# Attention with float32 probabilities and values, two heads side by side, and the value products of one group handed out between the scores of the next

## The chip, the cores and the metric

The kernel runs on one core of one Trainium2 chip. The metric is the device time of one execution in microseconds (us), the median over several runs. The core's engines are TensorE (PE, with its weight loads PEld), VectorE (DVE), ScalarE (ACT), GpSimd (POOL) and SyncE (SP); each works through its own instructions in a fixed order and waits for semaphores of the others.

## The reference

A chain of four layers over 1024 rows of width 1024. The part that the change touches is attention, in three places:

```
# memory attention (layers 0 and 1): 4 heads of 64, 256 memory rows
s = einsum('bqhd,bmhd->bhqm', q, mk) * HEAD_DIM ** -0.5
p = softmax(s);  out = einsum('bhqm,bmhd->bqhd', p, mv)
# grouped attention of layer 1: 12 query heads, 4 key heads of 64, 1024 rows, no mask
s = einsum('bqhgd,bkhd->bhgqk', qblk, k) * scale
p = softmax(s);  out = einsum('bhgqk,bkhd->bqhgd', p, v)
# latent attention (MLA) of the third layer: 8 heads, causal, 1024 rows, values of 64
s = where(mask, q_nope k_nope + q_rope k_rope, -inf) * scale
p = softmax(s);  out = einsum('bhqk,bkhd->bqhd', p, v)
```

Everything is float32, and the tolerance asks for more than one product in TensorE's rounded float32 format (fp32r in the rows) gives.

## The kernel before

The layers run one after the other: a long-convolution mixer with memory attention (layer 0), its experts, grouped attention with memory attention (layer 1), its experts, a recurrent layer with MLA, and a state-space layer (SSD). Most products are made of fp32r pieces: a number is split into a rounded high part and the rest (`K.split`, L127 to L134: ACT copies the high part, DVE or POOL subtracts), and pieces are multiplied in two or three passes.

**Grouped attention** (`Gqa.attend`, L1414). For each head, two groups of four tiles; a tile is 128 queries by all 1024 keys. Per tile: four score products into a two-bank PSUM tile `gs` (`scores`, L844: twice `gk`, twice `gkl`), the row maximum `mx` on DVE (L873), the exponential `prob` on ACT with the row sums `gsm` (L875), then eight 128x128 transposes `pT` on PE in two halves (L890), each followed by a split into `gph` (ACT) and `gpl` (DVE); one half in eight goes by way of ACT `pc` to POOL. After four tiles `out_heads` (L903) multiplies: values `vst` hold 64 high and 64 low columns side by side, so that one 128-column weight takes both, and per key tile there is one product with `gph` and one with `gpl`, 512 columns each, 16 per group of four tiles into the bank `ov`. ACT copies the two halves out, POOL adds them, and multiplies by `orc`: the reciprocals of the row sums, made rows by four transposes `rT` (L879) and an ACT copy (L921). One DMA stores 64 rows of `mixT`.

**Memory attention** (`Mem.attend`, L814) does the same per pair of heads with 256 columns: four tiles' transposes are split into `mph` and `mpl`, and each head has four products `ov` with `mv`. It stands between the projections of layers 0 and 1.

**MLA** (`Ab.mla_attend`, L1709) goes head by head; of each the four later query tiles, then the four earlier ones. Scores `as` come from three 96-row products and a mask product; the transposes `apT` are split into `aph` and `apl`; `mla_out` (L1776) multiplies with `mlv`, in narrowing column ranges where the mask cuts, and the result is divided by the sums and multiplied by the gate rows `ag` that a DMA has fetched. The splits of each head's queries and keys (`aql`, `akl`) run on POOL from the second head on.

PSUM banks: grouped attention has two for scores of two banks each, three for transposes (`tp`) and one for `ov`; MLA four, three and one. Buffers of the probabilities rotate by two.

The order in which the instructions of independent chains stand on each engine is set by a scheduler, which places them by its own estimates within what the data and the buffers allow; the program's order is its input, not its result. So an edit in the attention code can also move work of the next stage (here the weight pieces `pwh` and `pwl` of the layer's output product, which are prepared during the last heads of MLA).

Of the kernel before, what the change touches and what calls it, by code (L numbers as in the profile page):

```python
# [731 lines left out]
class Mem:  # L732
# [8 lines left out]
    def load(self, pool):  # L741

        K = self.K
        raw = K.raw(4, 256)
        K.nc.sync.dma_start(out=raw, in_=self.d.rearrange("b p n -> p b n"))
        for b in range(2):
            self.key_pair(pool, raw[:, b], 256, f"m{b}")
        self.v = pool.tile([P, 2, 4, P], F32R, name="mv")
        for b in range(2):
            self.values(b, raw[:, 2 + b])  # L750

    def values(self, b, src):
        self.K.split(self.v[:, b, :, 0:64], self.v[:, b, :, 64:128], src.rearrange("p (h d) -> p h d", h=4))

    def kv(self, pool, mt, wp, mem):
# [19 lines left out]
        if not self.layer:  # L775
            self.v = pool.tile([P, 2, 4, P], F32R, name="mv")
# [37 lines left out]
    def attend(self, wk, mixT, row0, pair, qs, tg, pk=None):  # L814

        K = self.K
        ph = wk.tile([P, 4, 256], F32R, name="mph", tag="mph")
        pl = wk.tile([P, 4, 256], F32R, name="mpl", tag="mpl")
        for tt in range(2):
            t = tg * 2 + tt  # L820
            ps = K.psum("ms", "s")
            for q in range(2):
                h = 2 * pair + q
                scores(K, ps[:, q * 256:(q + 1) * 256], qs[q][:, t * P:(t + 1) * P], self.k2[h], self.kl2[h])
            prob = softmax_rows(K, pk or wk, ps[:, 0:512], 2)
            pT(K, prob, ph, pl, tt)
        for q in range(2):
            h = 2 * pair + q
            out_heads(K, wk, ph, pl, [(2 * q + mb, self.v[:, mb, h]) for mb in range(2)],
                      mixT.piece(row0 + h * 64, row0 + h * 64 + 64, tg * 256, (tg + 1) * 256))  # L830
# [48 lines left out]
def columns_to_rows(K, ps, v):  # L879

    for j in range(v.shape[1]):
        K.transpose(ps[0:64, j * P:(j + 1) * P], v[:, j:j + 1].broadcast_to([P, 64]))


def pT(K, prob, ph, pl, tt, pool=None, off=()):

    nc = K.nc
    s = slice(tt * P, (tt + 1) * P)
    for h in range(0, prob.shape[1] // P, 4):
        ps = K.psum("pT", "tp")  # L890
        for k in range(4):
            K.transpose(ps[:, k * P:(k + 1) * P], prob[:, (h + k) * P:(h + k + 1) * P])
        v = ps[:, 0:512].rearrange("p (k t) -> p k t", k=4)
        if h in off:
            c = pool.tile([P, 4, P], F32, name="pc", tag="pc")
            nc.scalar.activation(out=c, in_=v, func=AF.Copy)
            nc.gpsimd.tensor_copy(out=ph[:, h:h + 4, s], in_=c)
            nc.gpsimd.tensor_tensor(out=pl[:, h:h + 4, s], in0=c, in1=ph[:, h:h + 4, s].bitcast(F32), op=OP.subtract)
        else:
            K.split(ph[:, h:h + 4, s], pl[:, h:h + 4, s], v)  # L900


def out_heads(K, pool, ph, pl, kv, dst, tag="tp", sums=None):  # L903

    nc = K.nc
    n = ph.shape[2]
    ps = K.psum("ov", tag)
    for j, (k, v) in enumerate(kv):
        K.mm(ps[:, 0:n], v, ph[:, k], j == 0, False)
        K.mm(ps[:, 0:n], v, pl[:, k], False, j == len(kv) - 1)  # L910
    o = pool.tile([64, n], F32, name="oh", tag="oh")
    nc.scalar.activation(out=o, in_=ps[64:128, 0:n], func=AF.Copy)
    o2 = pool.tile([64, n], F32, name="oh2", tag="oh2")
    nc.scalar.activation(out=o2, in_=ps[0:64, 0:n], func=AF.Copy)  # L914
    nc.gpsimd.tensor_tensor(out=o2, in0=o2, in1=o, op=OP.add)  # L915
    if sums is not None:
        nc.vector.reciprocal(out=sums, in_=sums)
        rp = K.psum("rT", "tp")
        columns_to_rows(K, rp, sums)
        r = pool.tile([64, n], F32, name="orc", tag="orc")  # L920
        nc.scalar.activation(out=r, in_=rp[0:64, 0:n], func=AF.Copy)  # L921
        nc.gpsimd.tensor_tensor(out=o2, in0=o2, in1=r, op=OP.mult)
    nc.sync.dma_start(out=dst, in_=o2)
# [383 lines left out]
class Gqa:  # L1307
# [50 lines left out]
    def results(self, pool, vpool):  # L1358

        self.qT = pool.tile([P, NH // 2, T], F32, name="qT")  # L1360
        self.kT = pool.tile([P, NKV // 2, T], F32, name="kT")
        self.v = vpool.tile([P, NT, NKV, P], F32R, name="vst")
# [5 lines left out]
    def project(self, u, ws, wk, uh, ul, t):  # L1368
# [6 lines left out]
        if u == 1:  # L1375
            p3 = ps[:, 0:256].rearrange("p (h d) -> p h d", h=4)
            K.split(self.v[:, t, :, 0:64], self.v[:, t, :, 64:128], p3)
            return
# [35 lines left out]
    def attend(self, wk, mixT, kpools, qp, op):  # L1414
        K = self.K
        for h in range(NH):
            kv = h // 3
            if h % 3 == 0:
                k2, kl = self.keys(kpools[kv % 2], kv)
            qs = self.stack(qp, h)  # L1420
            for tg in range(2):
                ph = wk.tile([P, 8, 512], F32R, name="gph", tag="gph")
                pl = wk.tile([P, 8, 512], F32R, name="gpl", tag="gpl")
                sm = K.small.tile([P, 4], F32, name="gsm", tag="gsm", bufs=2)
                for tt in range(4):
                    t = tg * 4 + tt
                    ps = K.psum("gs", "s")
                    scores(K, ps, qs[:, t * P:(t + 1) * P], k2, kl)
                    prob = exp_rows(K, wk, ps, sm[:, tt:tt + 1])
                    pT(K, prob, ph, pl, tt, wk, (4,) if tt == 2 else ())  # L1430
                out_heads(K, op, ph, pl, [(kb, self.v[:, kb, kv]) for kb in range(8)],
                          mixT.piece(h * 64, h * 64 + 64, tg * 512, (tg + 1) * 512), tag="ov", sums=sm)
# [81 lines left out]
class Ab:  # L1514
# [157 lines left out]
    def mla_heads(self, pools, rp, wk):  # L1672
# [5 lines left out]
        self.v = pools[2].tile([P, NT, 8, P], F32R, name="mlv")  # L1678
        uqh, uql = load_w(K, rp, a["mla_w_uq_2"][0], 0, 768, 2, "uq")
        ukh, ukl = load_w(K, rp, a["mla_w_ukv_2"][0], 0, 1024, 1, "uk")  # L1680
        for t in range(NT):
# [15 lines left out]
            K.split(self.v[:, t, :, 0:64], self.v[:, t, :, 64:128], v[:, :, 64:128])  # L1697
# [11 lines left out]
    def mla_attend(self, cp, wk, yT):  # L1709
# [7 lines left out]
        G.affine_select(out=msk, in_=z, pattern=[[-1, P]], compare_op=OP.is_ge, fill=-1e30, base=0, channel_multiplier=1)  # L1717
        for h in range(8):
# [4 lines left out]
            pp = []  # L1723
            for tg in range(2):
                pp.append([cp.tile([P, 4 + 4 * tg, 512], F32R, name=f"ap{x}{tg}") for x in "hl"])
            sm = K.small.tile([P, 2, NT], F32, name="asm", tag="asm", bufs=2)
            G.memset(sm[:, 1, 0:4], 0.0)
            todo = [4, 4]
            for t in (4, 5, 6, 7, 0, 1, 2, 3):
                p = self.mla_tile(wk, qk, t, idb, msk, sm)  # L1730
                q = t // 4
                self.mla_pT(p, pp[q], t)
                todo[q] -= 1
                if not todo[q]:
                    self.mla_out(wk, yT, h, q, *pp[q], sm[:, :, 4 * q:4 * q + 4])
# [28 lines left out]
    def mla_pT(self, p, pp, t):  # L1764

        K = self.K
        ph, pl = pp
        cs = slice(t % 4 * P, (t % 4 + 1) * P)
        for k0 in range(0, t + 1, 4):
# [4 lines left out]
            K.split(ph[:, k0:k0 + m, cs], pl[:, k0:k0 + m, cs], tp[:, 0:m * P].rearrange("p (k t) -> p k t", t=P))  # L1774

    def mla_out(self, wk, yT, h, tg, ph, pl, sm):  # L1776

        K, nc = self.K, self.K.nc
        gt = wk.tile([64, 512], F32, name="ag", tag="ag", bufs=1)
        dst = yT.piece(512 + h * 64, 512 + h * 64 + 64, tg * 512, (tg + 1) * 512)  # L1780
        nc.sync.dma_start(out=gt, in_=dst)
        rs = K.small.tile([P, 4], F32, name="ars", tag="ars", bufs=2)
        nc.vector.tensor_tensor(out=rs, in0=sm[:, 0], in1=sm[:, 1], op=OP.add)
        nc.vector.reciprocal(out=rs, in_=rs)
        rp = K.psum("rT", "tp")
        columns_to_rows(K, rp, rs)
        r = wk.tile([64, 512], F32, name="arb", tag="arb", bufs=1)
        nc.scalar.activation(out=r, in_=rp[0:64, 0:512], func=AF.Copy)
        nc.gpsimd.tensor_tensor(out=gt, in0=r, in1=gt, op=OP.mult)
        po = K.psum("ao", "ov")  # L1790
        nk = tg * 4 + 4
        for k in range(nk):
            c0 = max(0, k - tg * 4) * P
            K.mm(po[:, c0:512], self.v[:, k, h], ph[:, k, c0:512], k == 0, False)
            K.mm(po[:, c0:512], self.v[:, k, h], pl[:, k, c0:512], False, k == nk - 1)
        o = wk.tile([64, 512], F32, name="aoh", tag="aoh", bufs=1)
        nc.scalar.activation(out=o, in_=po[64:128, 0:512], func=AF.Copy)
        nc.vector.tensor_tensor(out=o, in0=po[0:64, 0:512], in1=o, op=OP.add)
        nc.gpsimd.tensor_tensor(out=o, in0=o, in1=gt, op=OP.mult)
        nc.sync.dma_start(out=dst, in_=o)  # L1800
# [538 lines left out]
```

## Time and profile before

| | |
|---|---|
| time, median of 3 runs | 3911.36 us (3908.62 to 3912.82) |
| the profiled execution: time | 3914.67 us |
| its span, first to last instruction | 3912.9 us |
| granted clock of TensorE, mean over the span | 0.955 of 2.4 GHz |
| grouped attention | 1624 to 1930 us |
| MLA attention | 2822 to 2984 us |

The page gives busy time per engine over the whole span. Since the stages have different limits, the views of stretches (busy time of each engine between two times) and the timeline of an engine (start, duration, line, operation, tile written <- tiles read, and in brackets the idle time before and what ended it) say more. Matmuls are pipelined: a matmul's recorded duration overlaps the next one, and what a matmul costs is the distance between two starts.

### The profile page before, as it was taken

Reading aid. Unit: us, or ns where it says so; the run is one execution under the profiler, and the core shown is the slowest. Engines: PE = TensorE matmul, PEld = TensorE weight load, DVE = VectorE, ACT = ScalarE, POOL = GpSimd, SP = SyncE. Lnnn points to the kernel's source line nnn. Section 1 sums busy time; section 2 is a strip of 40 time slices with the busy share of each in tenths; the row PEclk is TensorE's granted clock in tenths of the full one; section 3 lists DMA queues with packets and bytes.
Section 4 is the critical chain, followed back from the end, with each engine's and each line's share of the span. In section 5 each row is a group of like instructions: output and inputs, shape, how many; then the busy total and the mean of one; then the engine's idle time right before and its main releaser. Section 6 shows DMA issues by size and latency. Waiting matters only on the chain.

```text
span 3912.9 us, 52838 instructions
## 1 busy us (share of the span) xinstructions
PE 3554.6 (91%) x19679; PEld 3016.3 (77%) x19679; DVE 2877.1 (74%) x5200; ACT 1994.3 (51%) x2958; POOL 1055.1 (27%) x939
## 2 busy tenths in 40 slices
PE   7997999985999979899886999989998998999798
PEld 6885878764988969777766888868786876777577
DVE  6547878857998789777687988766476676667575
ACT  4433532223766754689734767645584234445330
POOL 2004745400453321244301554313352000000010
PEclk9998998997999999999997999989999999999899
DMA  4223333464999951000366999851114312222341
GB/s 156 92 83 109 116 130 113 134 201 169 361 361 355 356 195 34 16 12 12 99 227 230 375 358 346 306 157 48 43 39 128 105 56 81 69 77 92 108 156 65
DMA packets 205721, 603.64 MB, mean 154 GB/s; under 512 B 23110, under 2 KB 114104, under 8 KB 179865
## 3 DMA queue, kind: packets, MB, share of 16 engines
q1 hardware_dynamic: 193769, 558.58, 39.5%
q0 software_dynamic: 11696, 41.69, 4.1%
q8 instruction: 155, 2.54, 0.3%
q14 instruction: 101, 0.83, 0.1%
HBM read 503.60 MB, written 96.60 MB: 153 GB/s over the span
## 4 chain that ended last, share of the span: by engine, by line
PE 60%; DVE 11%; ACT 4%; DMA 2%; issue 2%; POOL 1%; SPq 0%; ACTq 0%; DVEq 0%; POOLq 0%
PE out L176 12%; PE gate L176 8%; PE xbc L176 7%; PE up L176 5%; PE z L176 5%; PE down L176 4%; DVE mwl L134 4%; PE ov L176 2%; PE pT L125 2%; PE gs L176 2%; PE yd L176 2%; PE as L176 1%; PE xr L176 1%; PE qk L176 1%; POOL mwl L134 1%
## 5 line engine op out<-in xcount | busy, mean ns | idle before, releaser
L134 DVE TENSOR_TENSOR mwl<-mwr,mwh 128x1024 fp32r<-128x1024 f32 x486 | 646.3, 1381 | 55.2 <-ACT mwh L130 54.4
L130 ACT ACTIVATE mwh<-mwr 128x1024 fp32r<-128x1024 f32 x576 | 563.0, 1050 | 52.5 <-PE up L176 28.8
L134 POOL TENSOR_TENSOR mwl<-mwr,mwh 128x1024 fp32r<-128x1024 f32 x90 | 257.5, 2887 | 272.2 <-ACT mwh L130 253.9
L1857 POOL DMA_DIRECT2D pyr<-y3T_d x31 | 23.5, 758 | 758.6 <-PE z L176 593.4
L1226 POOL DMA_INDIRECT xg<-xn_d,idx x32 | 58.9, 1839 | 467.2 <-DVE gsc L1224 466.7
L915 POOL TENSOR_TENSOR oh<-oh,oh 64x256 f32<-64x256 f32 (+1 forms) x56 | 55.2, 986 | 396.7 <-ACT oh L914 382.3
L134 DVE TENSOR_TENSOR gpl<-pT,gph 128x512 fp32r<-128x512 f32 x168 | 110.6, 684 | 40.8 <-ACT gph L130 26.8
L873 DVE TENSOR_REDUCE mx<-gs 128x1 f32<-128x1024 f32 x96 | 116.8, 1218 | 30.1 <-PE gs L176 29.8
L125 PE MATMUL pT<-ident,prob 128*128 128x128 f32 x896 | 126.6, 276 | 13.6 <-DVE gpl L134 8.2
L176 PE MATMUL gate<-mwh,xgl 128*128 128x384 f32 x512 | 137.3, 349 | 0.5 <-DVE xgl L134 0.4
L125 PEld LDWEIGHTS pT<-ident,prob 128*128 128x128 f32 x896 | 105.2, 141 | 39.4 <-ACT prob L875 6.7
L176 PE MATMUL gate<-mwl,xgh 128*128 128x384 f32 x512 | 134.7, 343 | 0.9 <-DVE mwl L134 0.8
L176 PE MATMUL gate<-mwh,xgh 128*128 128x384 f32 x512 | 134.2, 342 | 0.0
L176 PE MATMUL up<-mwl,xgh 128*128 128x384 f32 x512 | 132.0, 337 | 1.9 <-DVE mwl L134 1.9
L176 PE MATMUL up<-mwh,xgh 128*128 128x384 f32 x512 | 132.2, 338 | 0.0
L176 PE MATMUL up<-mwh,xgl 128*128 128x384 f32 x512 | 131.6, 337 | 0.0
L176 PE MATMUL down<-mwl,hh 128*128 128x512 f32 x384 | 122.6, 401 | 6.0 <-POOL mwl L134 6.0
L130 ACT ACTIVATE xgh<-xgT 128x512 fp32r<-128x512 f32 (+1 forms) x68 | 38.1, 566 | 173.7 <-PE xgT L125 173.1
L176 PE MATMUL out<-pwh,pyl 128*128 128x512 f32 x384 | 120.8, 396 | 6.3 <-DVE pyl L134 4.9
L176 PE MATMUL down<-mwh,hl 128*128 128x512 f32 x384 | 122.9, 400 | 0.0
L176 PE MATMUL out<-pwl,pyh 128*128 128x512 f32 x384 | 121.1, 396 | 0.0
L176 PE MATMUL out<-pwh,pyh 128*128 128x512 f32 x384 | 121.1, 396 | 0.0
(742 smaller groups left out, 11373.2 us busy)
## 6 DMA issues: line engine op xcount, KB each, us to landing
mwr<-in_exp_w_gate_dram SPq DMA_DIRECT2D x64, 1536.0 KB
mwr<-in_exp_w_up_dram SPq DMA_DIRECT2D x64, 1536.0 KB
mwr<-in_exp_w_down_dram SPq DMA_DIRECT2D x64, 1536.0 KB
csr<-cs_d SPq DMA_DIRECT2D x32, 512.0 KB
raw<-in_ssd_w_in_dram SPq DMA_DIRECT2D x15, 1024.0 KB
k_d<-kev SPq DMA_DIRECT2D x54, 256.0 KB
kt<-k_d SPq DMA_DIRECT2D x54, 256.0 KB
raw<-in_hy_w_in_dram SPq DMA_DIRECT2D x10, 1024.0 KB
```

The lines of the kernel that those rows point to most:

```text
L125: self.nc.tensor.transpose(out, in_, self.ident[:n, :n])
L130: nc.scalar.activation(out=hi, in_=src, func=AF.Copy)
L134: e.tensor_tensor(out=lo, in0=src, in1=hi.bitcast(F32), op=OP.subtract)
L176: self.nc.tensor.matmul(out=out, lhsT=lhsT, rhs=rhs, start=start, stop=stop)
L873: nc.vector.tensor_reduce(out=mx, in_=ps, axis=AX.X, op=OP.max, negate=True)
L915: nc.gpsimd.tensor_tensor(out=o2, in0=o2, in1=o, op=OP.add)
L1226: nc.gpsimd.indirect_dma_start(out=xg, out_offset=None, in_=self.xnD, in_offset=bass.IndirectOffsetOnAxis(ap=idx[:, 0:1], axis=0))
L1857: K.nc.gpsimd.dma_start(out=raw, in_=yT[q].rearrange("(p k) t -> p k t", k=self.kt)[:, :, t * P:(t + 1) * P])
```

## The change

Probabilities and values are no longer split. Values are float32 with 64 columns per head. After a transpose there is one copy: the first half of a grouped-attention tile goes to ACT, the second to DVE; memory attention's go to ACT; MLA's first key half goes to DVE, the other to ACT. The value products are float32 products with 64 weight columns; two heads write the two halves of the same bank (partitions 0 to 63 and 64 to 127), and stand alternately. The sums of a pair of heads are handled once: DVE reciprocal, a POOL copy that spreads them to 128x512 (`orcb`, `arbb`), four transposes, one ACT copy. One DVE multiplication then reads the bank and writes the result, in place of two ACT copies, a POOL addition and a POOL multiplication per head; MLA keeps one POOL multiplication with the gate. One DMA stores the 128 rows of the pair. In the program, the products of a group (two heads, 512 queries) are a generator of eight steps, and one step is taken after each tile of the next group.

```
-def pT(K, prob, ph, pl, tt, pool=None, off=()):
+def pT(K, prob, pt, tt, engs):
...
-            K.split(ph[:, h:h + 4, s], pl[:, h:h + 4, s], v)
+        if engs[h // 4] == "act":
+            nc.scalar.activation(out=pt[:, h:h + 4, s], in_=v, func=AF.Copy)
+        else:
+            nc.vector.tensor_copy(out=pt[:, h:h + 4, s], in_=v)
+def pair_rows(K, pool, sums, tag):
...
+    nc.vector.reciprocal(out=sums, in_=sums)
+    b = pool.tile([P, n, 2, 64], F32, name=tag + "b", tag=tag + "b", bufs=1)
+    nc.gpsimd.tensor_copy(out=b, in_=sums.rearrange("p n (q o) -> p n q o", o=1).broadcast_to([P, n, 2, 64]))
+    rp = K.psum("rT", "tp")
+    for j in range(n):
+        K.transpose(rp[:, j * P:(j + 1) * P], b[:, j].rearrange("p q d -> p (q d)"))
+    r = pool.tile([P, n * P], F32, name=tag, tag=tag)
+    nc.scalar.activation(out=r, in_=rp[:, 0:n * P], func=AF.Copy)
+    return r
-def out_heads(K, pool, ph, pl, kv, dst, tag="tp", sums=None):
+def out_pair(K, pt, vs, tag, done, cut=lambda k: 0):
...
+    for k in range(m):
+        c = cut(k)
+        for q in range(2):
+            K.mm(ps[q * 64:(q + 1) * 64, c:n], vs[q][k], pt[q][k][:, c:n], k == 0, k == m - 1)
+        if k == m - 1:
+            done(ps)
+        yield
 # Gqa.attend
+                for tt in range(4):
                     t = tg * 4 + tt
...
+                    for q in range(2):
+                        ps = K.psum("gs", "s")
+                        scores(K, ps, qs[q][:, t * P:(t + 1) * P], *kk[hs[q] // 3])
+                        prob = exp_rows(K, wk, ps, sm[:, tt, q:q + 1])
+                        pT(K, prob, pt[q], tt, ("act", "dve"))
+                        next(steps, None)
+                finish(steps)
+                steps = self.outputs(op, mixT, pr, tg, hs, pt, sm)
 # Gqa.outputs, once per group
+            r = pair_rows(K, op, sm, "orc")
+            o = op.tile([P, 512], F32, name="oh", tag="oh")
+            K.nc.vector.tensor_tensor(out=o, in0=ps[:, 0:512], in1=r, op=OP.mult)
 # Ab.mla_out
+        r = pair_rows(K, wk, rs, "arb")
         nc.gpsimd.tensor_tensor(out=gt, in0=r, in1=gt, op=OP.mult)
...
+            nc.vector.tensor_tensor(out=o, in0=po[:, 0:512], in1=gt, op=OP.mult)
```

Memory attention calls `out_pair` too and runs all its steps at once, into a `tp` bank, with one ACT copy per pair. `mla_attend` steps the generator twice after each of the earlier query tiles, once after each of the later ones.

What the scheduler makes of this on PE, in the middle of grouped attention (`gs` scores, `pT` transposes, `ov` value products; a row with x is that many in a run). Before, half of a head's products, the next tile and the other half's beginning:

```order
L176 MATMUL ov<-gph,vst 128x512
L176 MATMUL ov<-gpl,vst 128x512
L125 MATMUL pT<-ident,prob 128x128 x4
L176 MATMUL gs<-gk_16408,gqs 128x512 x2
L176 MATMUL gs<-gkl,gqs 128x512 x2
L176 MATMUL ov<-gph,vst 128x512
L125 MATMUL pT<-ident,prob 128x128 x4
L176 MATMUL ov<-gpl,vst 128x512
```

The piece of the changed program at the like place, with the last of 13 products of one group that stand directly after each other:

```order
L176 MATMUL ov<-gpt_16139,vst 64x512
L125 MATMUL pT<-ident,prob 128x128 x12
L176 MATMUL gs<-gk_15719,gqs 128x512 x2
L176 MATMUL gs<-gkl,gqs 128x512 x2
L176 MATMUL gs<-gk_15719,gqs 128x512 x2
L176 MATMUL gs<-gkl,gqs 128x512 x2
L176 MATMUL ov<-gpt_16140,vst 64x512
L176 MATMUL ov<-gpt_16139,vst 64x512
L176 MATMUL ov<-gpt_16140,vst 64x512
L125 MATMUL pT<-ident,prob 128x128 x12
```

So the 16 products of a group do not stand one pair after each tile: eight groups of the twelve have them as 13 and 3, one as 14 and 2, one as 12 and 4, the first as 1, 14 and 1, and the last as 16 at the end, 24 runs in all, nine of the groups with odd counts.

On DVE at the end of a group of the changed program (`gpt` copies, `gsm` reciprocal of the sums, `oh` the result):

```order
L877 TENSOR_REDUCE mx<-gs 128x1 x2
L910 COPY gpt_16139<-pT 128x4x128
L887 RECIPROCAL gsm<-gsm 128x8
L910 COPY gpt_16140<-pT 128x4x128
L877 TENSOR_REDUCE mx<-gs 128x1
L1452 TENSOR_TENSOR oh<-ov,orc 128x512
L877 TENSOR_REDUCE mx<-gs 128x1
```

The multiplication that empties the one `ov` bank stands on DVE among the row maxima; before, DVE had no part in emptying it.

On POOL in MLA (`arbb` the spread sums, `ag` the gate rows, `aql` and `akl` the next head's splits):

```order
L889 COPY arbb<-ars 128x512
L134 TENSOR_TENSOR aql<-mqT_25115,aqh 96x1024
L134 TENSOR_TENSOR akl<-mkT_25116,akh 96x1024
L1818 TENSOR_TENSOR ag<-arb,ag 128x512
L1752 MEMSET asm 128x8
L889 COPY arbb<-ars 128x512
L1818 TENSOR_TENSOR ag<-arb,ag 128x512
```

The gate multiplication, which the result waits for, stands in this turn behind both splits of the next head.

## Rows read from the trace of the kernel before

**Rows 1.** The page: busy time of each engine, share of the span, instructions.

```profile
PE 3554.6 (91%) x19679; PEld 3016.3 (77%) x19679; DVE 2877.1 (74%) x5200; ACT 1994.3 (51%) x2958; POOL 1055.1 (27%) x939
```

**Rows 2.** Stretches (start:end, length, then busy time of each engine, clock, DMA).

```profile
1624.20:1930.50 306.30, 287.87 (x1635) 235.03 (x1634) 226.25 (x296) 267.57 (x482) 132.18 (x114) 0.98 0.08 18
2821.60:2984.00 162.40, 144.14 (x896) 117.80 (x896) 124.16 (x281) 134.28 (x344) 81.08 (x53) 0.96 0.19 54
120.00:300.00 180.00, 180.00 (x860) 147.83 (x859) 96.18 (x129) 69.08 (x130) 10.39 (x14) 1.00 0.27 93
1424.00:1624.00 200.00, 175.53 (x1375) 168.56 (x1376) 173.37 (x539) 97.38 (x221) 43.88 (x43) 0.95 0.17 52
```

**Rows 3.** Timeline of PE in grouped attention (start, duration, line, operation).

```profile
1714.61 0.72 PE L176 MATMUL gs<-gk,gqs 128*128 128x512 f32 x2
1715.64 1.03 PE L125 MATMUL pT<-ident,prob 128*128 128x128 f32 x8
1716.43 0.72 PE L176 MATMUL gs<-gk,gqs 128*128 128x512 f32 x2
...
1720.19 0.60 PE L125 MATMUL rT<-ident,gsm 128*64 128x128 f32 x4
1720.55 0.49 PE L176 MATMUL ov<-gph,vst 128*128 128x512 f32 x1
...
1721.11 0.39 PE L176 MATMUL ov<-gph,vst 128*128 128x512 f32 x1
1721.34 0.39 PE L176 MATMUL ov<-gpl,vst 128*128 128x512 f32 x1
```

**Rows 4.** PE's largest wait from 1664 to 1904 us: total, times, longest.

```profile
PE pT L125 <- DVE gpl L134: 6.7, 13, 2.1
```

**Rows 5.** Timeline of PE between the layers: two float32 products, each recorded as two.

```profile
1418.97 1.98 PE L176 MATMUL x<-ye,ohf 128*128 128x512 f32 x4 [1.25 <-ACT ye L1289]
```

**Rows 6.** Timeline of PE in SSD: float32 products of two heads, side by side.

```profile
3659.30 0.40 PE L176 MATMUL z<-ul,wh 128*128 128x512 f32 x1
3659.63 0.44 PE L176 MATMUL yd<-csr,xs 128*64 128x128 f32 x4
...
3660.99 0.39 PE L176 MATMUL yd<-csr,xs 128*64 128x128 f32 x4
3661.31 0.50 PE L176 MATMUL z<-ul,wh 128*128 128x512 f32 x1
```

**Rows 7.** Groups of grouped attention: shapes, count, busy time, mean ns, idle before.

```profile
L873 DVE TENSOR_REDUCE mx<-gs 128x1 f32<-128x1024 f32 x96 | 116.8, 1218 | 30.1 <-PE gs L176 29.8
L134 DVE TENSOR_TENSOR gpl<-pT,gph 128x512 fp32r<-128x512 f32 x168 | 110.6, 684 | 40.8 <-ACT gph L130 26.8 <-issue 12.1
L875 ACT ACTIVATE prob<-gs,mx 128x1024 f32<-128x1024 f32 x96 | 107.1, 1116 | 6.0 <-DVE mx L873 4.4 <-POOL oh L915 0.9
L130 ACT ACTIVATE gph<-pT 128x512 fp32r<-128x512 f32 x168 | 93.6, 595 | 17.1 <-PE pT L125 16.0
L915 POOL TENSOR_TENSOR oh<-oh,oh 64x512 f32<-64x512 f32 x24 | 30.7, 1278 | 112.8 <-ACT oh L914 112.8
L1411 POOL TENSOR_TENSOR gqs<-qT,gqs 64x1024 fp32r<-64x1024 f32 x10 | 23.8, 2380 | 34.2 <-ACT gqs L1410 34.0
L897 POOL CAST gph<-pc 128x512 fp32r<-128x512 f32 x24 | 14.6, 610 | 17.4 <-ACT pc L896 17.2
```

**Rows 8.** Timeline of PE: the end of grouped attention, and the output product after it.

```profile
1926.79 0.39 PE L176 MATMUL ov<-gpl,vst 128*128 128x512 f32 x1
...
1936.56 0.80 PE L176 MATMUL out<-owh,mixl 128*128 128x512 f32 x1 [9.22 <-DVE mixl L134]
```

**Rows 9.** Timeline of PE in MLA: one head's wait, and the longest.

```profile
2871.49 0.45 PE L176 MATMUL as<-akh,aqh 96*128 96x384 f32 x1 [0.81 <-ACT aprob L1761]
...
2948.70 0.69 PE L176 MATMUL as<-akh,aqh 96*128 96x384 f32 x1 [5.77 <-ACT aprob L1761]
```

**Rows 10.** Groups of MLA: POOL's splits of the keys, one per head.

```profile
L134 POOL TENSOR_TENSOR akl<-mkT,akh 96x1024 fp32r<-96x1024 f32 x7 | 17.3, 2472 | 0.0
```

More of the change, by code (lines that the diff above doesn't have):

```diff
@@ L825, in attend, with done @@
             prob = softmax_rows(K, pk or wk, ps[:, 0:512], 2)
[L826 to L830, printed above, removed]
+            pT(K, prob, pt, tt, ("act",))
+        r0 = row0 + pair * P
+        def done(ps):
+            o = wk.tile([P, 256], F32, name="oh", tag="oh")
+            K.nc.scalar.activation(out=o, in_=ps[:, 0:256], func=AF.Copy)
+            K.nc.sync.dma_start(out=mixT.piece(r0, r0 + P, tg * 256, (tg + 1) * 256), in_=o)
+        finish(out_pair(K, [[pt[:, 2 * q + mb] for mb in range(2)] for q in range(2)],
+                        [[self.v[:, mb, (2 * pair + q) * 64:(2 * pair + q + 1) * 64] for mb in range(2)] for q in range(2)], "tp", done))
 def query_stack(K, s, ps, q):
@@ L876, in exp_rows @@
     return p
[L879 to L885 removed]
+def pair_rows(K, pool, sums, tag):
+    nc = K.nc
+    n = sums.shape[1]
+    nc.vector.reciprocal(out=sums, in_=sums)
[8 more added lines that the diff above has]
+def pT(K, prob, pt, tt, engs):
     nc = K.nc
@@ L893, in pT, with finish @@
         v = ps[:, 0:512].rearrange("p (k t) -> p k t", k=4)
[L894 to L898, printed above, removed]
-        else:
-            K.split(ph[:, h:h + 4, s], pl[:, h:h + 4, s], v)
-def out_heads(K, pool, ph, pl, kv, dst, tag="tp", sums=None):
-    nc = K.nc
-    n = ph.shape[2]
+        if engs[h // 4] == "act":
+            nc.scalar.activation(out=pt[:, h:h + 4, s], in_=v, func=AF.Copy)
+        else:
+            nc.vector.tensor_copy(out=pt[:, h:h + 4, s], in_=v)
+def out_pair(K, pt, vs, tag, done, cut=lambda k: 0):
+    n = pt[0][0].shape[1]
     ps = K.psum("ov", tag)
[L908 to L923, printed above, removed]
+    m = len(pt[0])
+    for k in range(m):
[5 more added lines that the diff above has]
+        yield
+def finish(steps):
+    for _ in steps:
+        pass
 NE = 16
@@ L1415, in attend @@
         K = self.K
[L1416 to L1420, printed above, removed]
+        kk = {}
+        steps = iter(())
+        for pr in range(NH // 2):
+            hs = (2 * pr, 2 * pr + 1)
+            for h in hs:
+                if h // 3 not in kk:
+                    kk[h // 3] = self.keys(kpools[h // 3 % 2], h // 3)
+            qs = [self.stack(qp, h) for h in hs]
             for tg in range(2):
-                ph = wk.tile([P, 8, 512], F32R, name="gph", tag="gph")
-                pl = wk.tile([P, 8, 512], F32R, name="gpl", tag="gpl")
-                sm = K.small.tile([P, 4], F32, name="gsm", tag="gsm", bufs=2)
+                pt = [wk.tile([P, 8, 512], F32, name=f"gpt{q}", tag=f"gpt{q}") for q in range(2)]
+                sm = op.tile([P, 4, 2], F32, name="gsm", tag="gsm", bufs=2)
@@ L1722, in mla_attend @@
                     K.split(qk[i][:, s], qk[i + 1][:, s], x[h // 4][0:96, h % 4, s], lo_eng="pool" if h else "dve")
[L1723 to L1735, printed above, removed]
+            q = h % 2
+            if q == 0:
+                pt = [[], []]
+                sm = cp.tile([P, 2, NT, 2], F32, name="asm", tag="asm", bufs=2)
+                G.memset(sm[:, 1, 0:4], 0.0)
+            for tg in (1, 0):
+                if q == 0:
+                    finish(steps)
+                    pt[tg] = [cp.tile([P, 4 + 4 * tg, 512], F32, name=f"ap{x}{tg}") for x in range(2)]
+                for t in range(4 * tg, 4 * tg + 4):
+                    p = self.mla_tile(wk, qk, t, idb, msk, sm[:, :, :, q])
+                    self.mla_pT(p, pt[tg][q], t)
+                    for _ in range(2 - tg):
+                        next(steps, None)
+                if q:
+                    finish(steps)
+                    steps = self.mla_out(wk, yT, h // 2, tg, pt[tg], sm[:, :, 4 * tg:4 * tg + 4])
+        finish(steps)
     def mla_tile(self, wk, qk, t, idb, msk, sm):
@@ L1803 @@
+        yield from out_pair(K, [[x[:, k] for k in range(n)] for x in pt], [[self.v[:, k, 2 * pr + q] for k in range(n)] for q in range(2)], "ov",
+                            done, lambda k: max(0, k - tg * 4) * P)
 class ProjNorm:
```

70 lines of the change are left out of this document (30 added, 40 removed).

## The prediction

> **What bounds the kernel now.** I read the page first: PE is busy for 91% of the span [rows 1]. That is an average, so the stretches of the stages came next. While grouped attention runs, PE is busy for 287.9 of 306.3 us, and the other engines have room, ACT least (267.6); in MLA PE has 144.1 of 162.4; a stretch of layer 0 with memory attention in it has PE busy all the time; only in the projections before grouped attention is DVE nearly level with PE, 173.4 and 175.5 of 200 us [rows 2]. Then I looked for what PE waits for: in 240 us of the middle of grouped attention its largest wait is 6.7 us in sum, for the DVE half of the split [rows 4]. So TensorE's own stream sets the pace there, and an edit that lightens ACT, DVE and POOL gains only where PE waits for them. The rest is in PE's timeline: what one tile's scores and transposes and one product cost [rows 3].
>
> **PE's stream in grouped attention.** One tile's scores take 1.03 us (1714.61 to 1715.64), its eight transposes 0.79 (to 1716.43), 1.82 in all; four transposes `rT` take 0.36, and a product `ov` of 512 columns 0.23 from start to start [rows 3]. Before: 96 tiles x 1.82 = 174.7, 384 products x 0.23 = 88.3, 24 x 0.36 = 8.6, together 271.6 us.
>
> After, there are 192 products in float32. Their price is in the trace elsewhere: two float32 products of 512 columns appear as four records of 1.98 us in all [rows 5]. With a last record of 0.4 to 0.7 us the starts lie 0.43 to 0.53 apart, so a product costs 0.86 to 1.05. I take 0.86: it is what four passes of 512 columns at the granted 2.4 GHz come to (4 x 0.213). The upper end would add 96 x 0.19 = 18 us. The Trainium skill says of true float32 that it takes four passes through the array ("FP8 and Floating Point Precision", TensorE Precision Notes); four times this trace's 0.23 would be 0.92 and add 6 us.
>
> Do two heads overlap? In SSD the float32 products of two heads stand side by side with 64 columns each: seven rows of four records (two products) start from 3659.63 to 3660.99, 0.227 apart, and with the neighbours the run takes 3661.31 - 3659.30 [rows 6]. Four passes of 128 columns are 4 x 128 / 2400 = 0.213 for one product alone. So the second head is free, and entering and leaving a run costs 2.01 - 0.23 - 7 x 0.227 = 0.2 us. Hence 96 pairs x 0.86 = 82.6. But the scheduler puts the products in 24 runs, 4.8 us, and in nine groups the runs have odd counts, where one product has no partner twice over: one extra slot each, 7.7 us. With 12 x 0.36 = 4.3 for `rT` the stream after is 274.1: **2.5 us more than before, not less.** Half the products, each nearly four times as long, two at a time, is a wash.
>
> **Waits in grouped attention.** What leaves the other engines is large: ACT loses 96 high copies and most result copies (per tile it has one exponential of 1.116 and one copy of 0.595, and a sum's readout), DVE swaps two 0.684 subtractions for one copy like them, POOL loses additions and multiplications [rows 7]. From the start at 1624.2 to the last product's end at 1927.2 [rows 2, 8] are 303 us, 31 more than the stream: so much at most is there to be won, and some of it is the filling of the pipeline.
>
> Against that stands the order. Before, each tile had its share of products behind it as cover for the chain scores, maximum (1.218), exponential (1.116), transposes. After, 13 products (5.8 us) stand together, and about six of eight tiles have no product near them. There PE has only 1.82 us per tile, while DVE needs 1.218 + 0.684 = 1.90 and ACT 1.116 + 0.595 + about 0.2 = 1.91, and `orc` and `gqs` on top make some 2.0. Six tiles x 0.2 = 1.2 us per group. The four `rT` now wait for reciprocal and a POOL copy (between the 0.610 of a POOL cast and the 1.278 of its addition), which can stand behind a query split of 2.380 [rows 7]: 0.4 per group. The one `ov` bank is emptied by a DVE multiplication (like a subtraction, 0.68) that needs `orc` and stands among the maxima; the next group's first product waits, 0.6. So 2.2 x 11 groups = 24. The first group has no products to cover it: 1.6 more. The start costs what it costs now, about 9 us. Sum 274.1 + 24 + 1.6 + 9 = 309, 6 more than 303. Bounds: if these waits vanish -14, if each doubles and products cost the upper end +30; the likely part is -14 to +20.
>
> **The end of the stage.** From the last `ov` PE is idle for 9.22 us until `out` [rows 8]; behind it stood two ACT copies, an addition and a multiplication on POOL and a DMA. One DVE multiplication instead saves 1 to 3 us, but 16 products now stand at the end, their sums at the front. I take -1. Grouped attention: +5.
>
> **MLA.** Counting columns in the same way, a head's products cost 4.2 us before: 33.6, with `rT` 39.4. After: in float32 the later query group of a pair costs 6.4 (5.6 and an unmatched product), the earlier 2.15, four pairs 34.3; 20 runs add 4.0, `rT` 2.9: 41.2, so +2. Waits: before, PE waits some 0.8 us per head for the exponential, and once 5.77 [rows 9]. ACT and DVE are lightened here too, -4. But the gate multiplication on POOL stands behind two splits of 2.47 us each [rows 10], the DVE multiplication waits for it, the bank for that, and the next products for the bank: 1.5 per pair, +6. Sum +4, bounds -9 (all waits gone, half of the 18 idle us) and +18 (a whole pair of splits, 4.9, in front of each of four banks).
>
> **Memory attention.** Eight products of 256 columns at 0.117 become two slots of 0.43 and a run's 0.2: 0.94 to 1.06. In layer 0, where PE is full [rows 2], eight attends give +1. In layer 1 DVE loses 16 subtractions of 0.68, 11 us of 173 [rows 2]; where it is the slower one, in part of the stretch, that shows: -2, bounds 0 and -8, less the same +1. The splits of the values become single copies, hidden behind products. Layer 1: -1.
>
> **Sum.** +5 + 4 + 1 - 1 = +9. The profiled execution took 3914.7 us, 3.3 above the median of 3911.4; the difference applies to either, so 3911.4 + 9 = **3920 us**. A measurement of this kernel can tell about 0.2%, 8 us: the forecast lies just beyond that.
>
> **The rivals.** *Faster: the lighter engines end the waits.* If the chain is short enough (ACT's next exponential no longer queues behind a high copy and result copies, so that transposes are ready whenever PE arrives), the order of the products doesn't matter, and the stages shrink to PE's stream and start: grouped attention -14 and its end -2, MLA -9, layer 1 -5, layer 0 +1: -29, 3882; with half of it, 3897. It decides at 1.82 us per tile: ACT and DVE must stay below. For it: ACT is busy for 87% of the stage and loses a third. Against: PE's largest wait sums to only 6.7 us in 240 [rows 4], and both engines stay at 1.9. Chance 0.30.
>
> *No change that can be told.* Half the waits I set appear, and ACT's relief pays the rest: 3904 to 3919. Chance 0.25.
>
> *The two heads overlap only in part*, so that the change doesn't do what it says. If not at all, 96 x 0.86 = 83 us more in grouped attention and 31 in MLA: 4034. The SSD rows speak plainly against it [rows 6], but their products have 128 columns, these 512. If a slot were a quarter longer, 0.25 x 117 = 29 us on top of the forecast: 3949. The Trainium skill has a measured speedup of 2.38 for three matmuls of 512 columns side by side, not 3 ("TensorE: Matmul & The Clock Gate", Part 3: Packing small matmuls — row/col tiling); as an estimate its ratio makes a slot 1.26 as long. Chance 0.05, the quarter included.
>
> My forecast, slower by waits at the clumps, has 0.40.
>
> **Numbers.** Faster 0.30, same 0.25, slower 0.45. The forecast's own range, from the bounds, is 3919 to 3945; the range that leaves out 2 in 10 reaches half into the faster case and stops short of the partial overlap: 3893 to 3946.
>
> **What would show it.** In the profile after: `ov` rows of 64 columns, two products (four records) per 0.86 us; ACT in the stage at some 175 us and DVE at some 190, against 267.6 and 226.3; POOL near 60. PE's waits before `pT` for the exponential in the stretches without products, above 15 us in the middle; `rT` waiting for POOL; `ov` waiting for the DVE result. In MLA, `ov` behind `ag`. Wrong would be: grouped attention ending before 300 us from its start (the rival), slots well over 0.86 (partial overlap), or the difference lying outside the attention stages, where the order of the instructions is the same as before.

## The result, and the profile after

The changed kernel takes **3934.3 us** (median of 4 runs, 3930.5 to 3941.2) against 3911.3 (4 runs, 3908.6 to 3912.8): 1.0062 times, 95% interval 1.0044 to 1.0079. It is 23 us slower, where +9 was forecast: the time lies in the stated range, and the loss is two and a half times the forecast.

Where the time went, from one profiled execution each (us between the first instructions of neighbouring stages on PE; grouped attention from its first score to the row `rgt` that opens the next stage):

| stretch | before | after |
|---|---|---|
| start to the first memory scores | 90.4 | 94.6 |
| layer 0 | 698.1 | 697.9 |
| its experts, projections of layer 1 | 835.9 | 833.2 |
| grouped attention | 302.7 | 323.4 |
| its output, experts of layer 1 (to the first `mc`) | 649.7 | 646.7 |
| recurrent layer up to MLA | 244.7 | 245.1 |
| MLA, to the output product | 165.9 | 164.7 |
| rest | 925.4 | 929.2 |
| span | 3912.9 | 3934.8 |

One stage holds nearly all of it. First the page after, then the stretches of grouped attention, MLA and the projections (start:end, length, busy time of PE, PEld, DVE, ACT, POOL, clock, DMA):

```profile
PE 3562.1 (91%) x19599; PEld 2942.2 (75%) x19599; DVE 2799.4 (71%) x5028; ACT 1864.6 (47%) x2658; POOL 904.1 (23%) x803
```

```profile
1626.20:1949.10 322.90, 290.62 (x1584) 186.39 (x1582) 194.05 (x224) 195.18 (x324) 33.14 (x25) 0.98 0.04 15
2841.00:3003.00 162.00, 143.94 (x864) 98.24 (x864) 104.13 (x223) 95.81 (x255) 52.28 (x33) 0.96 0.16 49
1424.00:1626.00 202.00, 179.56 (x1381) 166.92 (x1380) 158.80 (x519) 89.81 (x204) 31.02 (x30) 0.95 0.17 56
```

Against [rows 1, 2] every engine but PE is lightened as the diff promised: in grouped attention ACT falls from 267.6 to 195.2, DVE from 226.3 to 194.1, POOL from 132.2 to 33.1. PE's busy time is nearly the same (287.9 and 290.6), and the stage is 21 us longer. What PE waits for in it, in the same form as [rows 4] but over the whole stage:

```profile
PE pT L125 <- ACT prob L879: 27.8, 27, 3.0
PE gs L176 <- POOL gqs L1416: 2.8, 6, 1.1
PE gs L176 <- DVE gqs L1416: 2.7, 1, 2.7
PE ov L176 <- DVE oh L1452: 1.4, 1, 1.4
```

Before, the whole stage had this:

```profile
PE pT L125 <- DVE gpl L134: 8.2, 15, 2.1
PE pT L125 <- ACT prob L875: 5.3, 4, 2.9
...
PE gs L176 <- ACT prob L875: 1.3, 4, 0.6
...
PE ov L176 <- DVE gpl L134: 0.2, 1, 0.2
```

The 2.7 us for DVE's `gqs` stand before the stage's first score and belong to the stretch ahead of it. So 15.0 us of waits became 32.0, and these 17 us are most of the loss; the stage less its waits, PE's own time, went from 287.7 to 291.4. PE's timeline shows where the waits stand (answers to [rows 3]):

```profile
1788.97 1.04 PE L125 MATMUL pT<-ident,prob 128*128 128x128 f32 x8
1789.93 5.37 PE L176 MATMUL ov<-gpt,vst 128*64 128x512 f32 x24
1795.23 1.53 PE L125 MATMUL pT<-ident,prob 128*128 128x128 f32 x12
...
1798.52 1.94 PE L176 MATMUL ov<-gpt,vst 128*64 128x512 f32 x8
1800.39 1.53 PE L125 MATMUL pT<-ident,prob 128*128 128x128 f32 x12
...
1805.53 0.65 PE L125 MATMUL pT<-ident,prob 128*128 128x128 f32 x4 [0.88 <-ACT prob L879]
...
1809.82 1.09 PE L125 MATMUL pT<-ident,prob 128*128 128x128 f32 x8 [0.45 <-ACT prob L879]
...
1814.01 6.22 PE L176 MATMUL ov<-gpt,vst 128*64 128x512 f32 x26
1820.16 1.53 PE L125 MATMUL pT<-ident,prob 128*128 128x128 f32 x12
```

A float32 product is two records, so 24 are twelve products, in 5.30 us (1789.93 to 1795.23): six pairs of 0.86 and 0.14 for entry and exit. Thirteen take 6.15 (1814.01 to 1820.16), 0.85 more: a product without a partner costs as much as a pair, so two heads overlap fully at 512 columns. After the twelve come four products (1798.52 to 1800.39), and then only scores and transposes, with PE waiting for the exponential. ACT isn't the engine that is late: its own idle time before the exponential is a wait for DVE's maximum, which waits for the scores:

```profile
L879 ACT ACTIVATE prob<-gs,mx 128x1024 f32<-128x1024 f32 x96 | 106.9, 1114 | 38.1 <-DVE mx L877 37.5
L877 DVE TENSOR_REDUCE mx<-gs 128x1 f32<-128x1024 f32 x96 | 116.1, 1222 | 27.3 <-PE gs L176 26.7 <-ACT gpt L908 0.3
```

Scores, maximum, exponential and transposes wait for each other in turn, and the score banks come free only behind the exponential: a ring of latency that nothing else fills. At the end of the stage, PE's gap before `out` is 8.56 us where it was 9.22 [rows 8]; the four `rT`, 0.59 us, now stand between the last product and the gap:

```profile
1948.51 0.66 PE L125 MATMUL rT<-ident,orcb 128*128 128x128 f32 x4
...
1957.88 1.19 PE L176 MATMUL out<-owh,mixl 128*128 128x512 f32 x2 [8.56 <-DVE mixl L134]
```

In MLA the waits for the exponential keep their sum, 13.7 us after (the first rows) and 12.7 before (the second):

```profile
PE apT L125 <- ACT aprob L1791: 9.8, 13, 1.4
PE as L176 <- ACT aprob L1791: 3.9, 3, 2.1
...
PE ov L176 <- DVE aoh L1823: 1.5, 1, 1.5
```

```profile
PE as L176 <- ACT aprob L1761: 10.1, 7, 5.8
...
PE apT L125 <- ACT aprob L1761: 2.6, 3, 1.2
```

### The profile page after: what moved, and what is told of

The parts are those of the page before. It is cut to its first block, busy times and chain, and to the rows that moved or that the text cites. A ratio compares the mean times of both kernels' runs of the same rounds, so it can differ in the third digit from the quotient of the medians.

```text
span 3934.8 us, 51886 instructions
## 1 busy us (share of the span) xinstructions
PE 3562.1 (91%) x19599; PEld 2942.2 (75%) x19599; DVE 2799.4 (71%) x5028; ACT 1864.6 (47%) x2658; POOL 904.1 (23%) x803
## 4 chain that ended last, share of the span: by engine, by line
PE 61%; DVE 10%; ACT 3%; DMA 3%; issue 2%; POOL 1%; SPq 0%; ACTq 0%; DVEq 0%; POOLq 0%
PE out L176 11%; PE gate L176 8%; PE xbc L176 7%; PE up L176 5%; PE z L176 5%; DVE mwl L134 4%; PE down L176 4%; PE ov L176 3%; PE qk L176 2%; PE pT L125 2%; PE yd L176 2%; PE gs L176 2%; PE xr L176 1%; PE as L176 1%; ACT prob L879 1%
## 5 line engine op out<-in xcount | busy, mean ns | idle before, releaser
L176 PE MATMUL up<-mwl,xgh 128*128 128x384 f32 x512 | 132.2, 337 | 2.3 <-DVE mwl L134 2.3
L176 PE MATMUL up<-mwh,xgh 128*128 128x384 f32 x512 | 132.2, 338 | 0.0
L910 DVE COPY gpt<-pT 128x512 f32<-128x512 f32 x96 | 66.0, 688 | 87.3 <-PE pT L125 87.3
L879 ACT ACTIVATE prob<-gs,mx 128x1024 f32<-128x1024 f32 x96 | 106.9, 1114 | 38.1 <-DVE mx L877 37.5
L176 PE MATMUL xbc<-uh,wl 128*128 128x512 f32 x368 | 120.6, 404 | 0.0
```

The costliest lines, as they stand in the source:

```text
L176: self.nc.tensor.matmul(out=out, lhsT=lhsT, rhs=rhs, start=start, stop=stop)
L879: nc.scalar.activation(out=p, in_=ps, func=AF.Exp, bias=mx, accum_out=sm)
L910: nc.vector.tensor_copy(out=pt[:, h:h + 4, s], in_=v)
```

## The experiments

My theory after the trace: grouped attention loses because its products stand in clumps, so that most tiles have nothing on PE to cover their chain. Rivals: the rows of the sums, which now come late and hold the one product bank; or costs spread over the other places. Each experiment was timed in three rounds beside runs of the kernel before on the same chip; ratios are to those.

**1. Grouped attention undone.** In the changed kernel, `Gqa.results`, `project` and `attend` are those of the kernel before.

```
-        return out_pair(K, [[pt[q][:, kb] for kb in range(8)] for q in range(2)], ...
+                out_heads(K, op, ph, pl, [(kb, self.v[:, kb, kv]) for kb in range(8)],
+                          mixT.piece(h * 64, h * 64 + 64, tg * 512, (tg + 1) * 512), tag="ov", sums=sm)
```

> The changed kernel with grouped attention as before (split probabilities, values with 128 columns, one head at a time); memory attention and MLA stay changed. Theory (the loss arises in grouped attention): that stage goes back from 323 us (first score to last product's end) to about 303, the time to 3913 to 3917. Rival (the loss is spread over the other places or lies in the start of the program, where the changed kernel was 4 us late): the time stays above 3922.

Measured 3920.2, 1.0028 (1.0017 to 1.0040), between theory and rival. The stage goes back, to 299.9 us, but the time is some 10 us above the kernel before: another cost showed itself, which experiments 6 to 9 run down.

**2. Rows of the sums first.**

```
+        r = pair_rows(K, op, sm, "orc")
         def done(ps):
-            r = pair_rows(K, op, sm, "orc")
```

> The changed kernel, only with the sums of a group turned into rows (reciprocal, POOL copy, transposes, ACT copy) ahead of the group's products in the program and not behind them, so that the one product bank is emptied at once. Theory (the waits come from tiles without products near them, since the products still stand in clumps): within 8 us of the changed kernel, 3926 to 3942, PE's waits for the exponential still above 25 us in the stage. Rival (the late rows and the single bank cost the time): 10 to 20 us faster, 3914 to 3924.

3920.1, 1.0028 (1.0018 to 1.0038), the rival's time. The stage takes 316.1 us, 7 less than the changed kernel's; the waits for the exponential fall to 18.8:

```profile
PE pT L125 <- ACT prob L879: 18.8, 24, 2.8
```

My theory alone had said no change: a miss. But the stage holds only 7 of the 14 us by which this run is faster than the changed kernel; the profile has another 7 in the experts of layer 1 (640.1 against 646.7 us), which the edit doesn't touch (see experiment 11). Nor does the run set the late rows against the clumps: with the rows first, the scheduler also placed the products in 35 runs, where the changed kernel has 24. So late rows and the spread that comes with early ones are together worth a third of the stage's loss, and their shares were not tried apart.

**3. One pair per tile, and 4. two pairs per two tiles.** Rows first, and a one-column operation that adds zero times a tile's maximum to the probabilities which the pair reads. The sum is not altered; the pair becomes ready only when that tile's maximum is there, which keeps the scheduler from placing all products at once. The cut is that of 4; in 3 the operation and one step stand at each tile.

```
+                        if last and i % 2 == 1:
+                            for x in last:
+                                x = x[:, i - 1:i + 1, 0:1]
+                                K.nc.vector.scalar_tensor_tensor(out=x, in0=mx..., scalar=0.0, in1=x, op0=OP.mult, op1=OP.add)
                         pT(K, prob, pt[q], tt, ("act", "dve"))
-                        next(steps, None)
+                        if i % 2 == 1:
+                            for _ in range(2):
+                                next(steps, None)
```

> Rows first as in the run before, and each pair of products of a group is made to depend on the maximum of one tile of the next group (a one-column operation on DVE adds zero times that maximum to the first column of the probabilities that the pair reads), so that one pair stands beside each tile: about 100 runs of products in place of 24. Theory (clumps leave tiles uncovered): PE's waits for the exponential fall from 28 to below 10 us; 75 more runs at 0.2 us cost 15, seven odd slots fewer save 6: 3918 to 3930. Rival (the chain is not covered by products anyway, the order is indifferent): waits stay above 20 us and the runs cost on top, 3940 to 3955.

> As the run before, but two pairs of products after every second tile: 50 runs of four. Theory (clumps): half the cost of the runs, 5 us, and waits for the exponential below 14 us: 3912 to 3924, the fastest of the four with changed grouped attention. Rival (the order is indifferent): 3932 to 3945, waits above 25 us.

By pairs: 3924.4, 1.0043 (1.0026 to 1.0060), as the theory had it, the stage 318.7 us. Waits for the exponential:

```profile
PE pT L125 <- ACT prob L879: 4.2, 8, 1.5
```

The waits went, and the runs took it back: 101 runs where rows first alone had 35, and 15 us fewer waits for the exponential, yet the stage is 2.6 longer. A part of that is single products: 30 runs have an odd count, and one product (1703.81) takes as long as a pair (1705.39; a product is two records):

```profile
1703.81 1.07 PE L176 MATMUL ov<-gpt,vst 128*64 128x512 f32 x2
1704.81 0.66 PE L125 MATMUL pT<-ident,prob 128*128 128x128 f32 x4
1705.39 1.08 PE L176 MATMUL ov<-gpt,vst 128*64 128x512 f32 x4
1706.40 0.66 PE L125 MATMUL pT<-ident,prob 128*128 128x128 f32 x4
```

By fours, with 50 runs and 10 of them odd: 3917.3, 1.0013 (1.0004 to 1.0023). Its profile is of one of the fastest executions (3910.0) and has 305.8 us for the stage, 17.6 less than the changed kernel's:

```profile
PE ov L176 <- DVE gpt L1443: 7.0, 5, 1.9
PE pT L125 <- ACT prob L879: 4.9, 7, 1.9
PE gs L176 <- ACT prob L879: 3.1, 7, 0.8
```

That is as was expected: cover matters, and each run has its price. What is left against 302.7 is within what the added operation itself makes PE wait (7.0).

**5. Groups of half the size**, to shorten the fill: 256 queries, products of 256 columns, eight in a run.

```
-            for tg in range(2):
-                pt = [wk.tile([P, 8, 512], F32, ...
+            for tg in range(4):
+                pt = [wk.tile([P, 8, 256], F32, ...
```

> As the run with fours, but a group is two heads by 256 queries (four tiles) and not 512 (eight): products of 256 columns, eight in a run, half of a group's after its second and half after its fourth tile of the next. Theory (the rest of the loss against the kernel before is the longer fill and drain: the changed kernel scores for 24.5 us before its first product, where the kernel before took 16.7, and ends with 16 uncovered products): fill and end 8 to 11 us shorter than with fours, the time 3904 to 3912. Rival (fill and drain are hidden or the finer steps cost as much in runs, rows and copies): 3914 to 3924.

3934.5, 1.0045 (1.0027 to 1.0062): wrong in sign. The first product does come sooner, 18.9 us after the first score (28.6 with fours), but the stage takes 334.7 us, since both kinds of wait grow:

```profile
PE ov L176 <- DVE gpt L1443: 20.2, 11, 3.2
PE pT L125 <- ACT prob L879: 17.7, 22, 3.0
```

So the shorter fill is outweighed. That the products, which here wait for the second and the fourth tile's maximum, come too late for the tiles between is read from these rows and was not tried by itself.

**6. Only MLA changed, and 7. only memory attention changed**, all else as before.

```
 # 6: Ab.mla_heads, mla_attend, mla_pT, mla_out of the changed kernel; Mem and Gqa of the kernel before
 # 7: Mem.load, kv, values, attend of the changed kernel; Gqa and Ab of the kernel before
```

> The kernel before with the change in MLA alone. My step on record: +4 (bounds -9 to +18), 3915. Theory after the trace (MLA's stage is as long as before, 164.7 against 165.9 us to the output product): 3909 to 3914. Rival (the stretch after MLA, 2 to 4 us longer in all changed kernels, belongs to it): 3914 to 3919.

> The kernel before with the change in memory attention alone. My steps on record: +1 in layer 0 and -1 in layer 1, 3911. Theory: 3908 to 3914. Rival (the first 90 us, 2 to 4 us longer in all changed kernels, come from the values' single copies, which alter the order there): 3914 to 3918.

MLA alone: 3930.7 against 3915.7, 1.0039 (1.0025 to 1.0054), slower than either expectation. Memory attention alone: 3902.1, **0.9971** (0.9960 to 0.9982), faster than either expectation and than both kernels; where its 11 us lie is told at experiment 11.

MLA's stage is 166.8 us in run 6, 0.9 more than before, so its 15 us were elsewhere. TensorE's instructions outside of MLA and the transposes that prepare it stand in the same order as before, at a granted clock of 1.00 in the stretches compared, but the same products stand further apart in SSD and in the experts of both layers, which run before MLA. Runs 1 and 6 have this in common, and only they: two small tiles (the sums `asm` and their reciprocals `ars`) are no longer in the program-wide pool of small tiles, while grouped attention's `gsm` still is. So the next two runs move nothing but these.

**8. The sums moved, in the kernel before, and 9. their space kept, with MLA changed.**

```
 # 8, kernel before
-            sm = K.small.tile([P, 2, NT], F32, name="asm", tag="asm", bufs=2)
+            sm = cp.tile([P, 2, NT], F32, name="asm", tag="asm", bufs=2)
-        rs = K.small.tile([P, 4], F32, name="ars", tag="ars", bufs=2)
+        rs = wk.tile([P, 4], F32, name="ars", tag="ars", bufs=2)
 # 9, only MLA changed
+        for n, w in (("asm", 2 * NT), ("ars", 4)):
+            G.memset(K.small.tile([P, w], F32, name=n + "0", tag=n + "0", bufs=2), 0.0)
```

> The kernel before, word for word, with two small tiles (the row sums of MLA and their reciprocals) taken from the pools of the MLA stage and not from the program-wide pool of small tiles; TensorE's order is the same in every row. Theory (what MLA's run lost lies in where the other tiles come to lie: products of the same kinds stand 2% further apart there, 233 against 229 ns in SSD, 175.5 against 173 in the experts, in stages that the edit doesn't touch): 3924 to 3932, 10 to 18 us over the kernel before, with these distances. Rival (the MLA edit itself costs the time, the distances are the chip's): same as the kernel before within 6 us.

> The change in MLA alone, as in the run before that was 15 us slower, with two unused tiles of the old sums' size left in the program-wide pool, so that everything allocated after it lies where it lay. Theory (place of the tiles): the distances go back to 229 and 173 ns, and the time to within 6 us of the kernel before. Rival (the MLA edit costs the time): 10 to 20 us over the kernel before, as in that run.

Run 8: 3929.8 against 3915.4, 1.0040 (1.0028 to 1.0052). Run 9: 3918.8, 1.0006 (0.9996 to 1.0015). Both as the theory had it. A stretch of SSD's projection products on PE, in run 8 and then in the kernel before; sixteen take 3.73 us and 3.63:

```profile
3152.22 0.63 PE L176 MATMUL xbc<-ul,wh 128*128 128x512 f32 x2
3152.68 0.63 PE L176 MATMUL xbc<-uh,wh 128*128 128x512 f32 x2
...
3155.95 0.63 PE L176 MATMUL xbc<-uh,wl 128*128 128x512 f32 x2
```

```profile
3152.32 0.62 PE L176 MATMUL xbc<-ul,wh 128*128 128x512 f32 x2
3152.77 0.62 PE L176 MATMUL xbc<-uh,wh 128*128 128x512 f32 x2
...
3155.95 0.61 PE L176 MATMUL xbc<-uh,wl 128*128 128x512 f32 x2
```

So the change in MLA by itself costs 2 us (-2 to +6, from the ratio), and the 10 us of run 1 are no more than its tiles' place costs. The changed kernel doesn't pay this: its `xbc` products stand 228 ns apart, like those before. It moves all three kinds of sums.

**10. Memory attention and fours together**, MLA as before, the space of `gsm` kept, and before it grouped attention in fours alone.

```
 # fours alone: experiment 4's Gqa in the kernel before
 # together: and Mem of the changed kernel
+        K.nc.gpsimd.memset(K.small.tile([P, 4], F32, name="gsm0", tag="gsm0", bufs=2), 0.0)
```

> The kernel before with grouped attention alone changed, rows first and products in fours. Theory (what the other places cost adds up with grouped attention): the time with fours, 3917, less what MLA and memory attention cost by the run with grouped attention undone (9.5 us): 3906 to 3911. Rival (that run's 9.5 us come from the order of instructions elsewhere, which any edit shifts by some us): 3913 to 3920.

> The kernel before with the change in memory attention and, in fours with rows first, in grouped attention; MLA as before; an unused tile keeps the place of grouped attention's sums. If the runs with memory attention alone (11 us faster) and with grouped attention in fours alone (5 faster) add up: 14 to 18 us under the kernel before. Rival (both gain in the same place, DVE before grouped attention): 8 to 12 under it, no better than memory attention alone.

Fours alone: 3910.6, 0.9988 (0.9978 to 0.9998), the stage 301.2 us. Together: 3912.8, 0.9994 (0.9984 to 1.0003). The first lies in its theory's range, by luck: that took off the 9.5 us of run 1, which are tile places that run 4 doesn't pay for. The gains don't add up, and not even the rival's gain came; the stage takes 305.3 us there, as in run 4 with the changed memory attention. What both gain alone lies mostly in the experts of layer 1 (642.4 us in fours alone, 639.7 in memory attention alone, 649.7 before), and it can be had only once: 640.0 together.

**11. Only grouped attention changed**, as the change has it, the space of `gsm` kept.

```
 # Gqa of the changed kernel in the kernel before
+        K.nc.gpsimd.memset(K.small.tile([P, 4], F32, name="gsm0", tag="gsm0", bufs=2), 0.0)
```

> The kernel before with the change in grouped attention alone, as the change has it (rows of sums last, products in the scheduler's clumps), an unused tile keeping the place of its sums. Theory (the change's loss is this stage's): 16 to 26 us over the kernel before, the stage some 20 longer than 303, PE's waits for the exponential above 22 us. Rival (the waits come from what memory attention's new copies do to the start of the stage): below 12 us over.

3925.3 against 3913.8, 1.0030 (1.0019 to 1.0042), +11.5: between theory and rival. In the stage the theory holds: 324.9 us, 22 more than before, and

```profile
PE pT L125 <- ACT prob L875: 29.0, 28, 2.9
```

But 9 us come back in the experts after it (640.7 against 649.7 us), and 5 in layer 0, where TensorE's order is that of before: so much can differ between single executions. The experts' gain isn't the edit's. In fourteen profiles TensorE's order in the later part of those experts is that of before in the kernel before, the changed kernel and runs 6, 8 and 9, with 646.7 to 653.4 us; in the nine others the scheduler ordered it otherwise, with 636.2 to 643.3. Run 7 is one of the nine, with 639.7:

```profile
1927.11 0.22 PE L125 MATMUL rgt<-ident,rgr 8*128 8x8 f32 x1
...
2576.82 0.71 PE L176 MATMUL mc<-mh,ul 128*128 128x416 f32 x1 [1.06 <-DVE ul L134]
```

```profile
1917.96 0.22 PE L125 MATMUL rgt<-ident,rgr 8*128 8x8 f32 x1
...
2557.68 0.72 PE L176 MATMUL mc<-mh,ul 128*128 128x416 f32 x1 [1.07 <-DVE ul L134]
```

The first pair of rows is the kernel before, the second run 7. So 10 us of what run 7 wins go with an order that runs without memory attention's change show too. That the order is the reason was not tried by itself.

## Why the prediction was right in sign and short in size

- **What bounds the stage**: right. ACT lost 27% of its busy time in it and POOL 75%, and no time was won, since PE's stream and the ring scores to transposes set the pace.
- **PE's stream, "2.5 us more than before, not less"**: right in its difference: the stage less its waits is 287.7 us before and 291.4 after, 3.7 more. Two heads overlap at 512 columns, a pair costs 0.86, and the partial overlap fell. The estimate of 1.26 that was worked out from the Trainium skill's figure for three matmuls side by side ("TensorE: Matmul & The Clock Gate", Part 3: Packing small matmuls — row/col tiling) doesn't hold for these two: the trace has 0.86 us for a pair and 0.85 for a product alone.
- **Waits**: near in sum, 24 + 1.6 + 9 = 34.6 forecast, 32.0 measured, and that is partly luck. The largest kind was right, the exponential in the stretches without products, but it was priced at 1.2 us per group and took 2.2 (24.3 us behind the fill). Against that, no row shows `rT` waiting, which was priced at 0.4 per group; products waiting for the bank cost 1.4, not 6.6; and before the first product PE waits 4.7, not 9. The other engines were lightened otherwise than forecast: ACT to 195.2 us and not 175, POOL to 33.1 and not 60.
- **The step that failed**: "303 us, 31 more than the stream: so much at most is there to be won". I had read PE's waits in the middle [rows 4] and counted the stream from distances of equal instructions, and took all that remained as waits. Over the whole stage the waits of before are 15.0. The other 16 us are PE's own time, which the change leaves. Part of them is the start, at a granted clock of 0.85 of 2.4 GHz in the first 20 us; how the rest divides among the changes from one kind of matmul to the next was not measured. The forecast laid the new waits on a stream that was too short: 274.1 + 34.6 = 309, where 291.4 + 32.0 = 323.4 was measured. The same working on the busy time as it was, 287.7 + 2.5 + 34.6, gives +22 for the stage, and with the other terms as they stood +25, 3936 for the kernel.
- **MLA, +4**: the run alone shows +2 (-2 to +6); in the changed kernel's profile the stage is 1.2 shorter. The wait for the gate on POOL that I priced at 6 did not come (`ov` behind the DVE result 1.5 in all), and neither did the relief of 4: the waits for the exponential kept their sum.
- **Memory attention, 0 in sum**: about right in its own stretches. In the eight kernels with the change the projections of layer 1 (first `qk` to first score) take 181.8 to 185.3 us and in the six without it 187.8 to 191.1, some 5 less where 1 was forecast (DVE's busy time fell as forecast, from 173.4 to 158.8 in some 200 us); and the first memory scores come at 92.4 to 94.6 us instead of 89.0 to 91.0, some 3 later, where nothing was forecast. Layer 0 shows no difference beyond that of single executions. The 11 us that run 7 wins are for the most part not here but in the experts of layer 1.
- **The end of the stage, -1**: -0.7 by the gap, -0.1 from the last product's end, since the four `rT` come between.
- **What stays open**: by their ratios the single places add to 12 + 2 - 11 = 3 us (runs 11, 9 and 7), the whole change to 24 (17 to 31). By the profiles 16 of the 21 between them are the experts of layer 1, 10 us shorter in run 7 and 9 in run 11, and only 3 in the whole; the rest was not settled.

## What to carry to other kernels

Before you price a wait, split the stage into busy and idle with the waits of the whole stage, and lay changes on the busy time as it was measured, not on a sum of the smallest distances. When a pace is set by a ring of latency on a full engine, lighter neighbours win nothing, and work that served as cover must stay spread: a scheduler that takes all ready products at once undoes an interleaving that is only written in the program's order, while a dependency on the tile beside it (here one column) holds it, at the price of each run. And look where a single edit's gain lies before you keep it: memory attention alone takes 0.9971 of the time of before, but in its own stretches it wins some 2 us, and most of the rest is in a stage that the scheduler ordered otherwise.

## What was not expected of the hardware

Moving two tiles of 64 and 16 bytes per partition out of a pool that lives through the whole program, with TensorE's order unchanged, made products in other stages stand further apart: `xbc` and `z` of SSD 233 instead of 229 ns in the mean, `up` of the experts 176.0 instead of 173.3, while `out` of the third and fourth layer (231 and 232) and `proj` of the first (228) hardly changed. That was about 15 us of 3915, more than MLA's change by itself. It went away when the space was filled again. Which bytes must coincide was not tried; run 10's fours alone, with only `gsm` moved, show 229.4 and 173.6, so it isn't any shift whatever.
